# VectorE's order in the first stage of a retention and SSD block, written out by hand

## The chip, the cores and the metric

The kernel runs on one core of a Trainium2 chip. The metric is the time of one execution on the device in microseconds; the time before is the median of three runs. Its engines are TensorE (PE in the profile; PEld is its loading of weights), VectorE (DVE), ScalarE (ACT), GpSimd (POOL) and SyncE (SP), each with a queue of its own that it works off in order. The tile framework places the instructions: a scheduler takes the code's instructions with their dependences and priorities and fixes, when the kernel is built, the order on every engine.

## The reference, cut to what matters

One residual block on 512 tokens of width 2048: a normalization, one combined input projection, a retention branch (8 heads with rotary q and k), a Mamba-2 SSD branch, projections of both, gates, an output projection and a final normalization.

```python
def rmsnorm(x, w):
    xf = x.astype(f32)
    y = xf * lax.rsqrt(jnp.mean(xf * xf, axis=-1, keepdims=True) + EPS)
    return (y * w.astype(f32)).astype(x.dtype)

def rope(t, positions):
    half = t.shape[-1] // 2
    inv_freq = ROPE_THETA ** (-jnp.arange(half, dtype=f32) / half)
    ang = positions.astype(f32)[..., None] * inv_freq
    cos, sin = jnp.cos(ang)[:, :, None, :], jnp.sin(ang)[:, :, None, :]
    t1, t2 = t[..., :half], t[..., half:]
    return jnp.concatenate([t1 * cos - t2 * sin, t2 * cos + t1 * sin], axis=-1)
...
        h = rmsnorm(x, norm1_w[l])
        proj = jnp.einsum('bsd,de->bse', h, w_in[l])
        q, k, v, g_ret, z, xbc, dt_raw, gate_r, gate_s = jnp.split(proj, offsets, axis=-1)
        y_r = (retention(q, k, v, positions) * jax.nn.silu(g_ret.astype(f32))).astype(x.dtype)
        y_s = ssd(xbc, dt_raw, conv_w[l], conv_b[l], dt_bias[l], a_log[l], d_skip[l])
```

The order within the first stage matters here: the normalization of x, its split into operands for TensorE, the tables of cosine and sine (`rope`), the dt projection (`dt_raw`), and the first head's v, q, k and gate.

## The kernel before, in words

All projections are made in units of 256 output columns by 512 tokens, with features on the partitions. The 2048 features are eight *feature pairs* (`r0` to `r7`, each two rows of 128 features by 512 tokens). A number is held as a rounded high part and a low part that is the rest, and a product is three matmuls: high weight by high operand (L213), high by low (L214), low by high (L215). The weights of a unit come by `SP.dma_start` into `wf` (three buffers of two pairs); ScalarE casts the high part `whi` (L148) and VectorE subtracts for the low part `wlo` (L149), seven and six buffers.

A unit is either *plain* (12 matmuls of 512 columns per pair) or uses seven products in place of eight (21 matmuls of 256 columns per pair). The plain one needs only the *first half* of a pair's operand, tile `a` (rows 0 to 3: the difference of two rows, a cast, a low part). The seven-product unit also needs the *second half*, tile `b` (two sums and a difference into `g`, a cast, a low part), and combinations of the weights (L230, L232, L233 on VectorE). Each unit sums into four banks `pb0` to `pb3` of which there is one set, so the next unit's first product on a bank waits until VectorE and ScalarE have read that bank into `o`.

The first stage, in the code's order: `raw` pairs are loaded, ScalarE squares each, VectorE adds its two rows, TensorE sums over features with a matrix of ones (tile `att`); `inverse_root` gives `R1`; the dt weights `wdt` (in tile `e7`, loaded from ScalarE's queue) are scaled by the norm's weights and multiplied with the raw pairs; then each pair is scaled by weight and `R1`, and its first half is made. Head 0 follows with the units V (values), Q and K, all plain, and G (gate), which uses seven products and is the first to need second halves. `rotary_tables` makes the cosine and sine tables in 36 VectorE steps, a generator that the code advances with `step(n)`; `rotate` applies them to q and k, after which TensorE makes the scores.

Two things set the order here. Instructions issued through `InOrder` wrappers (`pe`, `act`, `dve`; in the profile they all have line L118, that of the helper) stay in the order of the code among themselves. Those issued through the plain names (`PE`, `ACT`, `DVE`) are placed where the scheduler finds them best. Before, `first_half` in this stage goes through `dve`, while the second halves and the rotary steps behind the root go through plain `DVE` (the class `Either` switches `vector.now` at the end of the first halves), so the scheduler mixes them in.

Transfers are counted on eight counters, dealt out in turn in the scheduler's order (in the rows below `DMAHW0_49` to `DMAHW7_49`). A transfer is issued only after the one before it on the same counter has landed; its engine's queue shows that as a wait ahead of the issue.

Of the kernel before, what the change touches and what calls it, by code (L numbers as in the profile page):

```python
# [8 lines left out]
F32 = mybir.dt.float32  # L9
# [7 lines left out]
P = 128  # L17
# [6 lines left out]
SH = 64  # L24
# [103 lines left out]
def hybrid_block(tc, A, out):  # L128
# [40 lines left out]
    def first_half(i, DVE=DVE, ACT=ACT):  # L169

        f, t = R[i], hp.tile([P, 8, 256], F32R, name=f"a{i}", tag=f"a{i}")
        X[i] = [t, None]
        DVE.tensor_tensor(f[:, 4, :], f[:, 0, :], f[:, 1, :], op=ALU.subtract)
        ACT.copy(t[:, 0:4, :], f[:, 1:5, :])
        DVE.tensor_tensor(t[:, 4:8, :], f[:, 1:5, :], t[:, 0:4, :].bitcast(F32), op=ALU.subtract)

    def second_halves(room):

        for i in range(NP):
            f, g = R[i], room[i % 2]  # L180
            DVE.tensor_tensor(g[:, 0:2, :], f[:, 0:5:4, :], f[:, 2:3, :].to_broadcast([P, 2, 256]), op=ALU.add)
            DVE.tensor_tensor(g[:, 2, :], f[:, 3, :], g[:, 1, :], op=ALU.subtract)
            t = X[i][1] = hp.tile([P, 6, 256], F32R, name=f"b{i}", tag=f"b{i}")
            split(t[:, 0:3, :], t[:, 3:6, :], g)

# [6 lines left out]
    def load_operands(src, n=NP):  # L192


        for i in range(NP):
            if i < n:
                SP.dma_start(out=raw_tile(i), in_=rows(src, i))
            first_half(i)

# [170 lines left out]
    act.dma_start(out=angles[:, 0, :].bitcast(I32), in_=A["positions"].partition_broadcast(P))  # L370
    act.dma_start(out=wdt, in_=w_in[:, DTO:DTO + SH].rearrange("(k p) c -> p k c", p=P))
    for i in range(NP):
        SP.dma_start(out=raw[i], in_=rows(A["xT"], i))
        if i == 0:
            SP.dma_start(out=cc, in_=A["consts"])

    class Either:

        now = dve

        def __getattr__(self, name):
            return getattr(self.now, name)

    vector = Either()
    steps = rotary_tables(angles, rooms[0][:, 6:8, :].rearrange("p h t -> p (h t)"), vector)

# [5 lines left out]
    act.activation(rstd[:, :1], eps, AF.Abs_reciprocal_sqrt)  # L392
    step(2)
    ps = att_tile()
    for i in range(NP):
        x, y = raw[i], early[i][:, 2 * T:].rearrange("p (r t) -> p r t", r=2)
        if i < NP - 1:
            act.activation(y, x, AF.Square)
            dve.tensor_tensor(y[:, 0, :], y[:, 0, :], y[:, 1, :], op=ALU.add)
            pe.matmul(ps, ones, y[:, 0, :], start=(i == 0), stop=False)  # L400
            step(1)
        else:
            for r in range(2):
                act.activation(y[:, r, :], x[:, r, :], AF.Square)
                pe.matmul(ps, ones, y[:, r, :], start=False, stop=(r == 1))

    dve.tensor_tensor(wdt, wdt, nw[:, :, None].to_broadcast([P, KD, SH]), op=ALU.mult)
    step(2)
    inverse_root(R1, ps, early[1][:, :T], early[2][:, :T], D, dve, act)
# [11 lines left out]

    for i in range(NP):
        for r in range(2):
            x, k = raw[i][:, r, :], 2 * i + r
            dve.scalar_tensor_tensor(x, x, nw[:, k:k + 1], R1, op0=ALU.mult, op1=ALU.mult)
        first_half(i, dve, act)
    vector.now = DVE

# [56 lines left out]
    with tc.tile_pool(name="ret", bufs=1) as rp:  # L485
# [3 lines left out]
        for h in range(NH):  # L489
# [30 lines left out]
            if h == 0:  # L520
                values()
                gs = rp.tile([P, 2, 3, 256], F32, name="g", tag="g")
                second_halves([gs[:, n] for n in range(2)])
                for _ in steps:
                    pass
            q = rotate(QO, qk[:, 0])
# [316 lines left out]
```

## Time and profile before

| what | us |
|---|---|
| time before, median of 3 runs | 2768.85 (2766.91 to 2770.41) |
| profiled execution, its own time | 2769.07 |
| its span | 2767.2 |
| TensorE busy | 2699.1 (98%) |
| VectorE busy | 2371.0 (86%) |
| ScalarE busy | 1343.0 (49%) |
| GpSimd busy | 175.2 (6%) |

The profile names instructions by line, engine, operation and tile, with buffer numbers left out; its records are of one execution. Rows of the timeline begin with the start and the length in us; an "x8" counts instructions that were merged into a row, and a bracket gives the idle time before and what ended it. Rows of waits give the total, the count and the longest. TensorE shows two records for a matmul in plain float32 and one for a rounded one.

### The profile page before, as it was taken

The numbers are of one execution on the slowest core, as the hardware profiler recorded it, in microseconds if no ns is written. First come the engines' busy times: TensorE is split into PE (matmuls) and PEld (weight loads), VectorE is DVE, ScalarE is ACT, GpSimd is POOL, SyncE is SP. The second block draws the span as 40 slices with busy tenths as digits, with TensorE's granted clock in tenths as the row PEclk, the third lists the DMA queues.
The fourth block names the chain that finished last, engine by engine and source line by source line (L and its number), as shares of the span: only waits on it lengthen the run. The fifth ranks groups of instructions, "written<-read, shape, count | busy, mean of one in ns | idle before, by whom it ended". The sixth has DMA issues, their size and how long they took to land.

```text
span 2767.2 us, 51984 instructions
## 1 busy us (share of the span) xinstructions
PE 2699.1 (98%) x20448; PEld 2567.6 (93%) x20448; DVE 2371.0 (86%) x3799; ACT 1343.0 (49%) x1923; POOL 175.2 (6%) x130
## 2 busy tenths in 40 slices
PE   6999999999999999999999999999999999999998
PEld 3799999999999999999999999999999989899898
DVE  8788888888878898898989888898889798898997
ACT  4334333343336555566565556556564353433453
POOL 0000000000000100000000000000000000011221
PEclk8999999999999999999999999999999999999999
DMA  4233333333333434343443434344464544557634
GB/s 141 77 96 92 115 100 107 96 100 103 104 112 107 141 108 127 121 129 121 128 142 120 136 108 128 116 132 126 131 200 144 192 155 141 179 169 230 203 123 138
DMA packets 339766, 362.46 MB, mean 131 GB/s; under 512 B 25152, under 2 KB 297792, under 8 KB 339520
## 3 DMA queue, kind: packets, MB, share of 16 engines
q1 hardware_dynamic: 319136, 325.05, 38.2%
q10 hardware_dynamic: 20384, 34.09, 3.3%
q8 instruction: 160, 2.62, 0.4%
q14 instruction: 86, 0.70, 0.1%
HBM read 321.56 MB, written 37.49 MB: 130 GB/s over the span
## 4 chain that ended last, share of the span: by engine, by line
PE 75%; DVE 11%; DMA 8%; issue 3%; ACT 1%; SPq 1%; POOL 0%; DVEq 0%; ACTq 0%; POOLq 0%
PE pb L215 21%; PE pb L214 21%; PE pb L213 20%; DVE wlo L149 3%; DMA wf<-in_w_in_dram 3%; DMA wf<-in_w_br_ssd_dram 2%; PE att L215 2%; PE att L214 2%; PE att L213 2%; PE att L549 1%; PE att L534 1%; DVE wf L230 1%; PE att L666 1%; PE pb L118 1%; PE att L670 1%
## 5 line engine op out<-in xcount | busy, mean ns | idle before, releaser
L148 ACT CAST whi<-wf 128x896 fp32r<-128x896 f32 (+1 forms) x968 | 818.5, 884 | 925.8 <-PE pb L214 390.0
L149 DVE TENSOR_TENSOR wlo<-wf,whi 128x896 fp32r<-128x896 f32 (+1 forms) x968 | 989.9, 1034 | 64.4 <-ACT whi L148 33.3
L213 PE MATMUL pb<-a,whi 128*128 128x256 f32 (+1 forms) x3328 | 1001.8, 304 | 13.7 <-ACT a L118 9.4
L214 PE MATMUL pb<-a,whi 128*128 128x256 f32 (+1 forms) x3328 | 1002.4, 302 | 8.7 <-DVE a L118 8.7
L215 PE MATMUL pb<-a,wlo 128*128 128x256 f32 (+1 forms) x3328 | 999.6, 302 | 5.9 <-DVE wlo L149 5.9
L213 PEld LDWEIGHTS pb<-a,whi 128*128 128x128 f32 x3328 | 636.7, 192 | 41.5 <-ACT a L118 13.3
L214 PEld LDWEIGHTS pb<-a,whi 128*128 128x128 f32 x3328 | 639.1, 192 | 33.9 <-DVE a L118 12.8
L215 PEld LDWEIGHTS pb<-a,wlo 128*128 128x128 f32 x3328 | 637.9, 192 | 29.9 <-DVE wlo L149 7.7
L213 PE MATMUL pb<-b,whi 128*128 128x256 f32 x2112 | 599.6, 284 | 0.0
L215 PE MATMUL pb<-b,wlo 128*128 128x256 f32 x2112 | 598.8, 284 | 0.0
L214 PE MATMUL pb<-b,whi 128*128 128x256 f32 x2112 | 598.0, 284 | 0.0
L230 DVE TENSOR_TENSOR wf<-wf 128x512 f32<-128x512 f32 x400 | 286.2, 715 | 185.3 <-DMA wf<-in_w_in_dram 138.7
L214 PEld LDWEIGHTS pb<-b,whi 128*128 128x128 f32 x2112 | 405.4, 192 | 0.1
L215 PEld LDWEIGHTS pb<-b,wlo 128*128 128x128 f32 x2112 | 405.3, 192 | 0.2
L213 PEld LDWEIGHTS pb<-b,whi 128*128 128x128 f32 x2112 | 405.4, 192 | 0.0
L233 DVE TENSOR_TENSOR wf<-wf 128x256 f32<-128x256 f32 x400 | 175.5, 439 | 3.4
L232 DVE TENSOR_TENSOR wf<-wf 128x256 f32<-128x256 f32 x400 | 174.5, 436 | 3.6
L215 PE MATMUL att<-a,wlo 128*128 128x256 f32 (+1 forms) x480 | 144.6, 306 | 5.3 <-DVE wlo L149 5.3
L213 PE MATMUL att<-a,whi 128*128 128x256 f32 (+1 forms) x480 | 145.5, 305 | 0.0
L214 PE MATMUL att<-a,whi 128*128 128x256 f32 (+1 forms) x480 | 145.3, 305 | 0.0
L215 PEld LDWEIGHTS att<-a,wlo 128*128 128x128 f32 x480 | 91.0, 192 | 10.3 <-DVE wlo L149 6.5
L659 ACT ACTIVATE L<-L,sst 128x128 f32<-128x128 f32 x256 | 78.5, 390 | 35.8 <-DMA L<-A_d 35.8
(221 smaller groups left out, 2736.6 us busy)
## 6 DMA issues: line engine op xcount, KB each, us to landing
wf<-in_w_in_dram SPq DMA_DIRECT2D x640, 256.0 KB, 3.1
wf<-in_w_br_ssd_dram SPq DMA_DIRECT2D x128, 256.0 KB, 3.4
wf<-in_w_out_dram SPq DMA_DIRECT2D x72, 256.0 KB, 3.2
wf<-in_w_in_dram SPq DMA_DIRECT2D x128, 128.0 KB, 2.6
L<-A_d SPq DMA_DIRECT2D x32, 512.0 KB, 3.7
wf<-in_w_br_ret_dram SPq DMA_DIRECT2D x64, 256.0 KB, 3.4
ys_d<-B ACTq DMA_DIRECT2D x32, 256.0 KB, 2.1
r<-ys_d SPq DMA_DIRECT2D x16, 512.0 KB, 6.1
```

The source lines that it names most:

```text
L118: ins = getattr(self.engine, name)(*args, **kw).ins
L148: ACT.copy(dst_hi, src)
L149: DVE.tensor_tensor(dst_lo, src, dst_hi.bitcast(F32), op=ALU.subtract)
L213: PE.matmul(o, wh, xh, start=b not in started, stop=False, skip_group_check=True)
L214: PE.matmul(o, wh, xl, start=False, stop=False, skip_group_check=True)
L215: PE.matmul(o, wl, xh, start=False, stop=(k == NP - 1), skip_group_check=True)
L230: DVE.tensor_tensor(f2[:, :, 4:6, :], f2[:, :, 1:3, :], f2[:, :, 0:1, :].to_broadcast([P, 2, 2, P]), op=ALU.subtract)
L232: DVE.tensor_tensor(f2[:, :, 0, :], f2[:, :, 2, :], f2[:, :, 4, :], op=ALU.add)
L233: DVE.tensor_tensor(f2[:, :, 6, :], f2[:, :, 3, :], f2[:, :, 0, :], op=ALU.subtract)
L534: PE.matmul(ps[:, :n], k[:, i, sb * P:(sb + 1) * P], q[:, i, sb * P:], start=(i == 0), stop=(i == 1))
L549: PE.matmul(ps[:, :DK], pt[sb][:, (lb - sb) * P:(lb - sb + 1) * P], v[:, sb, :], start=(sb == 0), stop=(sb == lb))
L659: ACT.activation(L[:, i, c, :], L[:, i, c, :], AF.Relu, scale=-1.0, bias=At[:, c, h0 + i:h0 + i + 1])
```

## The change

The order on VectorE is written out. `first_half` and the new `second_half` become generators that stop before and after the low part. After the root, a pair ahead is scaled, subtracted and cast while the low part of the pair before is made, all through `dve`. Second halves and four rotary steps in turn follow through `dve` behind all first halves, after V's code. One rotary step less is taken ahead of the squares, none beside pair 0, and the two steps ahead of the root are gone. The load of `wdt` moves from the head of ScalarE's queue to behind pair 4's square.

```diff
     def first_half(i, DVE=DVE, ACT=ACT):
...
         DVE.tensor_tensor(f[:, 4, :], f[:, 0, :], f[:, 1, :], op=ALU.subtract)
         ACT.copy(t[:, 0:4, :], f[:, 1:5, :])
+        yield
         DVE.tensor_tensor(t[:, 4:8, :], f[:, 1:5, :], t[:, 0:4, :].bitcast(F32), op=ALU.subtract)
+        yield
+
+    def second_half(i, g, DVE=DVE, ACT=ACT):
+
+        f = R[i]
+        DVE.tensor_tensor(g[:, 0:2, :], f[:, 0:5:4, :], f[:, 2:3, :].to_broadcast([P, 2, 256]), op=ALU.add)
+        DVE.tensor_tensor(g[:, 2, :], f[:, 3, :], g[:, 1, :], op=ALU.subtract)
+        t = X[i][1] = hp.tile([P, 6, 256], F32R, name=f"b{i}", tag=f"b{i}")
+        ACT.copy(t[:, 0:3, :], g)
+        yield
+        DVE.tensor_tensor(t[:, 3:6, :], g, t[:, 0:3, :].bitcast(F32), op=ALU.subtract)
+        yield
 
     def second_halves(room):
-
         for i in range(NP):
-            f, g = R[i], room[i % 2]
...
-            split(t[:, 0:3, :], t[:, 3:6, :], g)
+            list(second_half(i, room[i % 2]))
...
-            first_half(i)
+            list(first_half(i))
...
     act.dma_start(out=angles[:, 0, :].bitcast(I32), in_=A["positions"].partition_broadcast(P))
-    act.dma_start(out=wdt, in_=w_in[:, DTO:DTO + SH].rearrange("(k p) c -> p k c", p=P))
...
-    steps = rotary_tables(angles, rooms[0][:, 6:8, :].rearrange("p h t -> p (h t)"), vector)
+    steps = rotary_tables(angles, rooms[0][:, 6:8, :].rearrange("p h t -> p (h t)"), dve)
...
-    step(2)
+    step(1)
     ps = att_tile()
     for i in range(NP):
...
-            step(1)
+            if i:
+                step(1)
+            if i == 4:
+                act.dma_start(out=wdt, in_=w_in[:, DTO:DTO + SH].rearrange("(k p) c -> p k c", p=P))
...
     dve.tensor_tensor(wdt, wdt, nw[:, :, None].to_broadcast([P, KD, SH]), op=ALU.mult)
-    step(2)
     inverse_root(R1, ps, early[1][:, :T], early[2][:, :T], D, dve, act)
...
-    for i in range(NP):
+    def normalized(i):
         for r in range(2):
             x, k = raw[i][:, r, :], 2 * i + r
             dve.scalar_tensor_tensor(x, x, nw[:, k:k + 1], R1, op0=ALU.mult, op1=ALU.mult)
-        first_half(i, dve, act)
-    vector.now = DVE
+        yield from first_half(i, dve, act)
+
+    ahead = [normalized(i) for i in range(NP)]
+    next(ahead[0])
+    for i in range(NP):
+        if i + 1 < NP:
+            next(ahead[i + 1])
+        next(ahead[i])
...
                 values()
                 gs = rp.tile([P, 2, 3, 256], F32, name="g", tag="g")
-                second_halves([gs[:, n] for n in range(2)])
-                for _ in steps:
-                    pass
+                ahead = [second_half(i, gs[:, i % 2], dve) for i in range(NP)]
+                next(ahead[0])
+                for i in range(NP):
+                    if i + 1 < NP:
+                        next(ahead[i + 1])
+                    next(ahead[i])
+                    step(4)
+                step(99)
```

Three places in the built order. Names have their buffer's number behind them; the changed kernel's lines are eight and more further down (L213 to L215 become L221 to L223, L534 becomes L545). First, ScalarE at the start, before, with what each row waits for:

```order
L118 DMA B8_122<-in_positions_dram 128x512
L118 DMA e7_112<-in_w_in_dram 128x16x64
L118 ACT_TABLE_LOAD
L118 ACTIVATE rstd_80<-eps_91 128x1 [waits Pool_49]
L118 ACTIVATE e0_105<-r0_113 128x1024 [waits DMAHW2_49]
```

and changed, from pair 4's square (the rows between are the same):

```order
L118 ACTIVATE e4_109<-r4_117 128x1024 [waits DMAHW7_49]
L118 DMA e7_112<-in_w_in_dram 128x16x64 [waits DMAHW4_49]
L118 ACTIVATE e5_110<-r5_118 128x1024 [waits DMAHW0_49]
L118 ACTIVATE e6_111<-r6_119 128x1024 [waits DMAHW1_49]
L118 ACTIVATE e7_112<-r7_120 128x512 [waits DMAHW2_49]
L118 ACTIVATE e7_112<-r7_120 128x512
L148 CAST whi_257<-wf_254 128x512 [waits DMAHW3_49]
L148 CAST whi_273<-wf_254 128x512
L148 CAST whi_292<-wf_289 128x512 [waits DMAHW5_49]
L148 CAST whi_308<-wf_289 128x512 [waits DMAHW6_49]
L118 ACTIVATE e1_106<-att_135,eps_91 128x512 [waits PE_49]
L148 CAST whi_327<-wf_324 128x512 [waits DMAHW0_49]
```

The dt weights' load now has a wait, and three squares, the first weight casts and the root's activation stand behind it. On SyncE, before, the rows that tell the counters are

```order
L373 DMA r6_119<-in_xT_dram 128x2x512 [waits DMAHW2_49]
L373 DMA r7_120<-in_xT_dram 128x2x512 [waits DMAHW3_49]
L227 DMA wf_258<-in_w_in_dram 128x2x256 [waits DMAHW4_49]
L227 DMA wf_258<-in_w_in_dram 128x2x256 [waits DMAHW5_49]
L435 DMA na_1115<-in_a_log_dram 128x64 [waits DMAHW4_49]
```

and changed

```order
L380 DMA r6_119<-in_xT_dram 128x2x512 [waits DMAHW1_49]
L380 DMA r7_120<-in_xT_dram 128x2x512 [waits DMAHW2_49]
L235 DMA wf_254<-in_w_in_dram 128x2x256 [waits DMAHW3_49]
L235 DMA wf_254<-in_w_in_dram 128x2x256 [waits DMAHW4_49]
L441 DMA na_1115<-in_a_log_dram 128x64 [waits DMAHW3_49]
```

Before, counter 3 was that of the dt weights' load, and the last pair `r7` waits for it. Now the load comes after `na` in the dealing, so it has counter 4, whose last user is the second transfer of the first weight tile.

Second, VectorE behind the root (`R1`), before:

```order
L118 SCALAR_TENSOR_TENSOR R1_81<-R1_81,e1_106 128x512
L347 TENSOR_TENSOR B8_122<-B8_122,A8_121 128x512
L118 SCALAR_TENSOR_TENSOR r0_113<-r0_113,nw_76,R1_81 128x512 x2
L337 CAST B8_122<-B8_122 128x512
L118 TENSOR_TENSOR r0_113<-r0_113 128x256
L419 COPY rstd_80<-att_196 128x4
L338 TENSOR_TENSOR B8_122<-B8_122 128x512
L181 TENSOR_TENSOR g_417<-r0_113 128x512
L344 TENSOR_SCALAR B8_122<-B8_122 128x512
L118 TENSOR_TENSOR a0_204<-r0_113,a0_204 128x1024
L118 SCALAR_TENSOR_TENSOR r1_114<-r1_114,nw_76,R1_81 128x512 x2
L182 TENSOR_TENSOR g_417<-r0_113,g_417 128x256
```

and changed, from the fifth weight's low part:

```order
L149 TENSOR_TENSOR wlo_328<-wf_324,whi_327 128x512
L149 TENSOR_TENSOR wlo_344<-wf_324,whi_343 128x512
L118 TENSOR_TENSOR e7_112<-e7_112,nw_76 128x1024
L118 TENSOR_SCALAR e2_107<-att_135 128x512
L118 TENSOR_TENSOR R1_81<-e1_106 128x512
L118 SCALAR_TENSOR_TENSOR R1_81<-R1_81,e2_107 128x512
L118 SCALAR_TENSOR_TENSOR R1_81<-R1_81,e1_106 128x512
L118 SCALAR_TENSOR_TENSOR r0_113<-r0_113,nw_76,R1_81 128x512 x2
L118 TENSOR_TENSOR r0_113<-r0_113 128x256
L118 SCALAR_TENSOR_TENSOR r1_114<-r1_114,nw_76,R1_81 128x512 x2
L118 TENSOR_TENSOR r1_114<-r1_114 128x256
L118 TENSOR_TENSOR a0_200<-r0_113,a0_200 128x1024
```

Rotary steps (on `A8`, `B8`) and second halves (on `g`) are gone from between the pairs, and six weights' low parts stand ahead of the scaling of the dt weights (`e7`), which stood ahead of all of them.

Third, TensorE at the scores of head 0 (`att<-B8`), before, at the first of their two places, among the products of pairs 2 and 3 of G (`pb2_818`, `pb3_819`):

```order
L214 MATMUL pb3_819<-b2_430,whi_882 128x256
L534 MATMUL att_800<-B8_122 128x512
L534 MATMUL att_804<-B8_122 128x384
L534 MATMUL att_808<-B8_122 128x256
L534 MATMUL att_812<-B8_122 128x128
L215 MATMUL pb3_819<-b2_430,wlo_883 128x256
```

and changed, where `pb0_1177` is the first bank of the unit behind G:

```order
L221 MATMUL pb0_1177<-a2_211,whi_1243 128x256
L222 MATMUL pb0_1177<-a2_211,whi_1243 128x256
L545 MATMUL att_800<-B8_122 128x512 x2
L545 MATMUL att_804<-B8_122 128x384 x2
L545 MATMUL att_808<-B8_122 128x256 x2
L545 MATMUL att_812<-B8_122 128x128 x2
L223 MATMUL pb0_1177<-a2_211,wlo_1244 128x256
```

The scores moved from inside G to behind it and eight products of the next unit.

More of the change, by code (lines that the diff above doesn't have):

```diff
@@ L174, in first_half @@
         ACT.copy(t[:, 0:4, :], f[:, 1:5, :])
+        yield
         DVE.tensor_tensor(t[:, 4:8, :], f[:, 1:5, :], t[:, 0:4, :].bitcast(F32), op=ALU.subtract)
+        yield
[8 more added lines that the diff above has]
+        yield
     def second_halves(room):
         for i in range(NP):
-            f, g = R[i], room[i % 2]
-            DVE.tensor_tensor(g[:, 0:2, :], f[:, 0:5:4, :], f[:, 2:3, :].to_broadcast([P, 2, 256]), op=ALU.add)
-            DVE.tensor_tensor(g[:, 2, :], f[:, 3, :], g[:, 1, :], op=ALU.subtract)
-            t = X[i][1] = hp.tile([P, 6, 256], F32R, name=f"b{i}", tag=f"b{i}")
-            split(t[:, 0:3, :], t[:, 3:6, :], g)
+            list(second_half(i, room[i % 2]))
     def pair_rows(f):
@@ L375, in hybrid_block @@
             SP.dma_start(out=cc, in_=A["consts"])
[L377 to L384, printed above, removed]
-    steps = rotary_tables(angles, rooms[0][:, 6:8, :].rearrange("p h t -> p (h t)"), vector)
+    steps = rotary_tables(angles, rooms[0][:, 6:8, :].rearrange("p h t -> p (h t)"), dve)
     def step(n):
```

## The prediction

> **What bounds the kernel now.** I read the page first, then TensorE's waits by stretch, then the stretches themselves, then the first 85 us instruction by instruction. The page's span and busy row:
>
> ```profile
> span 2767.2 us, 51984 instructions
> PE 2699.1 (98%) x20448; PEld 2567.6 (93%) x20448; DVE 2371.0 (86%) x3799; ACT 1343.0 (49%) x1923; POOL 175.2 (6%) x130
> ```
>
> TensorE is busy for all but 68 us, so only a stretch in which it waits or runs slowly can give much. Such a stretch is the first unit, V. Its waits, then (third row) all that TensorE waits for from 84.5 to 300 us:
>
> ```profile
> PE pb L213 <- ACT a L118: 9.4, 7, 2.5
> PE pb L214 <- DVE a L118: 8.7, 7, 1.9
> ...
> PE pb L215 <- DVE wlo L149: 1.3, 1, 1.3
> ```
>
> The stretches (columns: length, busy time and count of PE, PEld, DVE, ACT, POOL, granted clock, DMA share, GB/s):
>
> ```profile
> 29.50:33.10 3.60, 1.10 (x10) 0.97 (x8) 3.60 (x8) 1.63 (x2) 0.00 (x0) 1.00 0.29 100
> 33.10:84.50 51.40, 35.74 (x96) 23.20 (x97) 49.26 (x81) 20.95 (x28) 0.00 (x0) 0.77 0.10 31
> 84.50:107.00 22.50, 22.50 (x104) 18.71 (x103) 9.15 (x16) 6.77 (x13) 0.00 (x0) 1.00 0.23 71
> 107.00:129.00 22.00, 22.00 (x98) 18.21 (x97) 18.08 (x31) 7.61 (x11) 0.00 (x0) 1.00 0.32 96
> 129.00:153.50 24.50, 24.50 (x186) 22.88 (x185) 20.30 (x33) 7.64 (x10) 0.00 (x0) 1.00 0.28 86
> ```
>
> In V (33.1 to 84.5) VectorE is busy 49.26 of 51.40 us, TensorE 35.74 at a clock of 0.77. VectorE is the bound there, and nowhere else near: the Q, K and G units that follow keep TensorE full at clock 1.00. The three rows of waits say the same: 18.1 us in V, 1.3 in the next 215. So the forecast is a date: the first product of Q, at 84.54 now. TensorE's order behind the first two heads is the same but for a late stretch in the output projection, so the end moves by what that date moves, less any wait newly made behind it.
>
> **The change, part by part.** One: the dt weights' load leaves the head of ScalarE's queue. What it did there, and what stands around it:
>
> ```profile
> SPq L373 <- DMA e<-in_w_in_dram: 6.6, 1, 6.6
> ...
> e<-in_w_in_dram ACTq DMA_DIRECT2D x1, 512.0 KB, 12.9
> ```
> ```profile
> 1.18 0.47 ACTq L118 DMA_DIRECT2D e<-in_w_in_dram  x1
> 15.22 1.06 ACT L118 ACTIVATE e<-r 128x1024 f32<-128x1024 f32 x1 [0.36 <-DMA r<-in_xT_dram]
> 16.56 1.06 ACT L118 ACTIVATE e<-r 128x1024 f32<-128x1024 f32 x1 [0.29 <-DMA r<-in_xT_dram]
> 19.29 1.15 ACT L118 ACTIVATE e<-r 128x512 f32<-128x512 f32 x2 [0.32 <-DMA r<-in_xT_dram]
> 19.75 2.84 PE L118 MATMUL att<-e,cc 128*128 128x512 f32 x6 [0.23 <-DVE e L118]
> 20.22 1.22 DVE L118 TENSOR_TENSOR e<-e,nw 128x1024 f32<-128x1024 f32 x1
> 20.35 2.54 ACT L148 CAST whi<-wf 128x512 fp32r<-128x512 f32 x4
> 21.36 0.42 DVE L118 CAST B<-B 128x512 int32<-128x512 f32 x1
> 22.53 7.09 PE L118 MATMUL att<-r,e 128*64 128x512 f32 x32
> 22.80 0.68 ACT L118 ACTIVATE e<-att,eps 128x512 f32<-128x512 f32 x1
> 23.64 1.32 ACT L148 CAST whi<-wf 128x512 fp32r<-128x512 f32 x2 [0.16 <-DMA wf<-in_w_in_dram]
> 28.64 0.68 DVE L118 SCALAR_TENSOR_TENSOR R<-R,e 128x512 f32<-128x512 f32 x1
> 29.55 1.05 PE L118 MATMUL att<-cc,R 128*128 128x2 f32 x8
> 33.12 1.85 PE L213 MATMUL pb<-a,whi 128*128 128x512 f32 x4 [2.52 <-ACT a L118]
> ```
>
> The load took 12.9 us beside the features, in 256-byte rows, and SyncE waited 6.6 us for it before it could issue the last feature pair, since a transfer is issued only when the one before it on its counter has landed. In the changed order the load stands behind the square of pair 4, and the counter that it gets was last used by the second transfer of the first weight tile (the orders above). So ScalarE, in its queue's order, stops at this issue until that transfer has landed. When is that? Feature pairs land 1.34 to 1.37 us apart (starts 15.22, 16.56, 19.29 of squares that wait for them: 4.07 for three), so half a megabyte taken out from between them is worth 1.4 us; 2.8, an estimate, if the load's 256-byte rows move at half that pace. I take 2.0. The last pair then lands at 19.29 - 2.0 = 17.3 and two quarter-megabyte transfers later, at 18.7, ScalarE goes on: issue 0.47, 19.2. Pair 5 was squared at 16.56, so the squares of the last three pairs are 2.6 us late: done at 19.2 + 2 x 1.06 + 1.15 = 22.5.
>
> TensorE has by then had nothing for about 5 us. What a wait does to its pace is seen at the start of V:
>
> ```profile
> 36.17 0.63 PE L215 MATMUL pb<-a,wlo 128*128 128x512 f32 x1
> 36.60 0.50 PE L214 MATMUL pb<-a,whi 128*128 128x512 f32 x1
> 36.94 0.39 PE L215 MATMUL pb<-a,wlo 128*128 128x512 f32 x1
> 37.17 0.39 PE L214 MATMUL pb<-a,whi 128*128 128x512 f32 x1
> 84.54 0.44 PE L213 MATMUL pb<-a,whi 128*128 128x512 f32 x1
> ```
>
> Starts lie 0.43 apart until 36.60, then 0.34, then 0.23: after the wait before 33.12 the products ran at half pace for 3.5 us, a loss of 1.75. [...]
>
> Bounds for the sum of squares: pair 5's sum starts at 19.2 + 1.06 + 0.7 = 20.95, and four sums at 0.9 (19.75: three in 2.84) end at 24.6, at half pace throughout at 28.2; with a loss of 1.75, at 26.4. Then the root's activation (0.2 + 0.68), two weight casts (1.32) and their low part on VectorE (0.1 + 0.60), because six low parts now stand ahead of the dt weights' scaling: 29.35. The load, issued at 19.2, lands by 32.1 if it takes 12.9 again; its neighbours now have 1 KB rows instead of 2 KB and there are fewer of them, so I take about 8 and do not let it decide; 32.1 stays as an end. So scaling starts at 29.35 (27.5 to 32.1), where it was 20.22: the start loses 9 us.
>
> Two: from there VectorE is free of the rest. Scaling 1.14 (20.22 to 21.36), three steps of the root at 0.60 and one of 0.68: R1 at 33.0 instead of 29.3. TensorE: dt product from 30.7, 7.02 (22.53 to 29.55) + 1.75 for the clock, then 1.05: first product of V at 40.5, against 33.12.
>
> Three: V itself. VectorE's work for a pair, start to start:
>
> ```profile
> 39.60 1.21 DVE L118 TENSOR_TENSOR a<-r,a 128x1024 fp32r<-128x1024 f32 x1
> 40.73 1.40 DVE L118 SCALAR_TENSOR_TENSOR r<-r,nw,R 128x512 f32<-128x512 f32 x2
> 42.06 0.68 DVE L149 TENSOR_TENSOR wlo<-wf,whi 128x512 fp32r<-128x512 f32 x1
> 42.66 0.41 DVE L182 TENSOR_TENSOR g<-r,g 128x256 f32<-128x256 f32 x1
> 43.60 0.41 DVE L118 TENSOR_TENSOR r<-r 128x256 f32<-128x256 f32 x1
> 43.93 0.68 DVE L149 TENSOR_TENSOR wlo<-wf,whi 128x512 fp32r<-128x512 f32 x1
> ```
>
> Low part 1.13, normalizing two rows 1.33, a weight's low part 0.60, difference 0.33: 3.4 us per pair, 8 x 2.79 + 6 x 0.60 = 25.9 from 33.0, last low part at 58.9. Before, a pair took 51.40 / 8 = 6.4 us because second halves and rotary steps lay between. TensorE's 96 products at 0.23 take 22.1: 40.5 + 22.1 = 62.6, later than VectorE's 58.9 plus the last eight products (1.8). So TensorE is the later one, no longer waits, and stays at full pace. Q's first product needs the first bank emptied; VectorE comes to it after the first second half, 0.60 + 0.33 + 0.60 + 0.60 + 0.33 + 0.87 + 0.60 + 0.42 behind 58.9 with one wait for V's seventh pair, about 63.5. **Gain so far: 84.54 - 63.5 = 21.0.**
>
> Four: what was moved must be done somewhere.
>
> ```profile
> L149 DVE TENSOR_TENSOR b<-g,b 128x768 fp32r<-128x768 f32 x8 | 7.6, 946 | 0.9 <-ACT b L148 0.9
> L181 DVE TENSOR_TENSOR g<-r 128x512 f32<-128x512 f32 x8 | 5.4, 677 | 0.0
> L182 DVE TENSOR_TENSOR g<-r,g 128x256 f32<-128x256 f32 x8 | 3.3, 410 | 0.0
> ```
>
> Second halves: 7.6 + 5.4 + 3.3 = 16.3. Rotary steps behind V: 29 by the changed order, 18 long at 0.68 and 11 short at 0.41, 16.7. Records overlap by 0.08, so 33.0 less 53 x 0.08: 28.8 us of VectorE. They are covered by its idle time in Q, K and G: 22.50 - 9.15, 22.00 - 18.08 and 24.50 - 20.30 make 21.5. The rest, 7.3, is still owed when G ends. But TensorE's order now has the scores of the first head behind G and eight products of the next unit, not inside G. Adding up starts along the changed order, the rotated k is ready 1 us after TensorE comes to the scores, and a second wait of about 1 stands at the first head's transposes. I take 2 us, between 0 and 7.3; the low end because the weights' parts, on which the products wait, stand interleaved with the moved steps and come in time by 2 to 8 us. ScalarE's casts of the second halves fall into a stage where it is busy 6.77 to 7.64 of 22 to 24.5 us and cost nothing. SyncE's weight loads follow the freeing of buffers as before; GpSimd's queue is unchanged.
>
> Sum, against the profiled execution's 2769.07 (0.22 above the median of 2768.85): -21.0 + 2 = -19.0, **2750**.
>
> **The rivals.** *ScalarE is not held by the load's issue.* Then the squares end at 18.6, and the sixth weight's low part and the load decide: about 26 instead of 29.35, 3.4 us earlier, 2746.7. For it: no row shows ScalarE waiting to issue; against: SyncE's 6.6 us. [...]
>
> *The moved work finds only part of the room.* VectorE's idle time in Q and K is waiting inside its own order, for TensorE, and a step that stands behind such a wait can't use it. With 5.5 us more to wait than I take, all the 7.3: 2755.5; with a few more, 2760.
>
> *The same, to the full, ends slower.* Place: the rotation of q and k, ahead of the scores. If none of the 21.5 us could be used, TensorE would wait all 28.8: 2769.07 - 21.0 + 28.8 = 2777. It turns slower by 0.2% when the waits pass 26.5. Against it: the moved steps stand between the waits, most of them with no wait of their own.
>
> *TensorE keeps V's mean pace*, because something other than the waits slows it. 35.74 us busy for 96 products is 0.37 each; V would take 35.7 from 40.5, Q come at 77, and the end at 2769.07 - 7.5 + 2 = 2763.5; at half pace throughout, 41.3 and 2769. For it: the clock of 0.77 beside waits of 2.5 us at most. Against it: rows 36.17 to 36.94, where 3.5 us without a wait end the half pace, and the clock of 1.00 in all stretches that do not wait. [...] That the change doesn't do what it says is excluded by the order.
>
> **How the numbers follow.** Forecast 0.66, unheld ScalarE 0.14, part of the room 0.11, V's mean pace 0.05, slower 0.04. The ends: start at 27.5 and no new wait, 2750 - 1.9 - 2 = 2746, or 2745 with the unheld ScalarE; start at 32.1 and all of 7.3, 2750 + 2.75 + 5.3 = 2758. Differences under 0.2% (5.5 us, about what a measurement of this kernel tells from none) are "same": faster 0.90, same 0.06, slower 0.04.
>
> **What would show it.** Right: a wait of ScalarE of 4 to 5 us before the square of pair 5; the scaling of the dt weights near 29; first product of V near 40, its clock near 1.00; Q's first product near 63.5; TensorE's wait for rotated k under 3 us. Wrong: TensorE waiting in V for features again, or waits for VectorE in K and G adding up to more than 7.

## The result, and the profile after

The changed kernel takes 2748.91 us (median of 6 runs, 2745.81 to 2755.9) where the kernel before takes 2767.4 (6 runs, 2765.62 to 2770.41): ratio 0.9939, 95% interval 0.9927 to 0.9951. The forecast was 2750, range 2745 to 2758. The profiled execution of after is its longest, 2755.9 us, so its late stages are not typical; the first 300 us, on which the forecast rests, are read from it.

The page's span and busy row, then how the start went (timeline: start, length, engine, line, operation; in brackets the idle time before it and what ended it):

```profile
span 2754.0 us, 51975 instructions
PE 2691.5 (98%) x20448; PEld 2565.0 (93%) x20448; DVE 2368.3 (86%) x3799; ACT 1342.7 (49%) x1923; POOL 179.3 (7%) x130
```
```profile
18.39 0.39 ACTq L118 DMA_DIRECT2D e<-in_w_in_dram  x1
18.83 3.04 ACT L118 ACTIVATE e<-r 128x1024 f32<-128x1024 f32 x4 [5.01 <-DMA wf<-in_w_in_dram]
20.66 6.51 PE L118 MATMUL att<-e,cc 128*128 128x512 f32 x8 [4.94 <-DVE e L118]
28.44 1.29 DVE L149 TENSOR_TENSOR wlo<-wf,whi 128x512 fp32r<-128x512 f32 x2 [3.53 <-ACT whi L148]
29.65 1.22 DVE L118 TENSOR_TENSOR e<-e,nw 128x1024 f32<-128x1024 f32 x1
30.92 9.88 PE L118 MATMUL att<-r,e 128*64 128x512 f32 x32 [3.75 <-DVE e L118]
41.65 1.18 PE L221 MATMUL pb<-a,whi 128*128 128x512 f32 x4
...
65.30 0.50 PE L221 MATMUL pb<-a,whi 128*128 128x512 f32 x1 [1.62 <-DVE o L270]
```

ScalarE stops 5.01 us, not for its own data but for a weight transfer (`wf`), and goes on when it has issued the dt weights' load at 18.39. The squares, their sum (20.66), the scaling (29.65, before: 20.22), the dt product and V's first product (41.65, before: 33.12) are late one after the other. Yet Q's first product comes at 65.30, where it came at 84.54. In between, the stretches of V, Q, K and G and the attention behind them (columns as before the change: length, busy time and count of PE, PEld, DVE, ACT, POOL, clock, DMA share, GB/s) and all that TensorE waits for from 64 to 300 us:

```profile
41.60:63.50 21.90, 21.90 (x98) 17.97 (x97) 20.87 (x34) 10.70 (x15) 0.00 (x0) 1.00 0.24 73
63.50:86.00 22.50, 20.88 (x96) 17.25 (x96) 21.33 (x38) 8.48 (x14) 0.00 (x0) 1.00 0.23 71
86.00:108.00 22.00, 22.00 (x98) 18.22 (x98) 21.69 (x39) 9.46 (x13) 0.00 (x0) 1.00 0.31 96
108.00:128.00 20.00, 20.00 (x161) 19.65 (x161) 19.57 (x33) 8.38 (x10) 0.00 (x0) 1.00 0.33 100
128.00:160.00 32.00, 29.38 (x208) 26.66 (x207) 26.80 (x57) 13.97 (x20) 2.20 (x4) 1.00 0.23 70
```
```profile
PE att L572 <- ACT yn L570: 2.0, 3, 1.1
PE pb L221 <- DVE o L270: 1.6, 1, 1.6
PE pb L221 <- ACT o L274: 0.9, 1, 0.9
```

V is now 21.9 us long, full, at clock 1.00 (before: 51.4 us, 35.74 busy, 0.77). VectorE, which was busy for 9.15 us of 22.5 in Q and 18.08 of 22 in K, is now busy 21.33 of 22.5 there and 21.69 of 22: the second halves and the rotary steps are done where TensorE has work of its own. For that TensorE waits 4.5 us behind V up to 300 us, 1.3 before.

### The profile page after: what moved, and what is told of

Read it like the earlier page. It is cut to its first block, busy times and chain, and to the rows that moved or that the text cites. A ratio compares the mean times of both kernels' runs of the same rounds, so it can differ in the third digit from the quotient of the medians.

```text
span 2754.0 us, 51975 instructions
## 1 busy us (share of the span) xinstructions
PE 2691.5 (98%) x20448; PEld 2565.0 (93%) x20448; DVE 2368.3 (86%) x3799; ACT 1342.7 (49%) x1923; POOL 179.3 (7%) x130
## 4 chain that ended last, share of the span: by engine, by line
PE 78%; DVE 9%; DMA 6%; issue 3%; ACT 1%; SPq 1%; POOL 0%; DVEq 0%; ACTq 0%; POOLq 0%
PE pb L223 21%; PE pb L221 21%; PE pb L222 21%; DMA wf<-in_w_in_dram 3%; DVE wlo L149 3%; PE att L222 2%; PE att L223 2%; PE att L221 2%; PE att L545 1%; DVE wf L238 1%; PE att L560 1%; PE att L677 1%; DMA wf<-in_w_br_ssd_dram 1%; PE att L681 1%; PE pb L118 1%
## 5 line engine op out<-in xcount | busy, mean ns | idle before, releaser
L221 PE MATMUL pb<-a,whi 128*128 128x256 f32 (+1 forms) x3328 | 998.3, 303 | 7.7 <-DVE o L277 4.3
L223 PE MATMUL pb<-a,wlo 128*128 128x256 f32 (+1 forms) x3328 | 994.5, 301 | 7.2 <-DVE wlo L149 7.1
L221 PEld LDWEIGHTS pb<-a,whi 128*128 128x128 f32 x3328 | 636.0, 191 | 32.3 <-issue 7.4
L223 PEld LDWEIGHTS pb<-a,wlo 128*128 128x128 f32 x3328 | 635.2, 191 | 30.4 <-DVE wlo L149 8.9
L221 PE MATMUL pb<-b,whi 128*128 128x256 f32 x2112 | 600.1, 284 | 0.0
L223 PE MATMUL pb<-b,wlo 128*128 128x256 f32 x2112 | 599.0, 284 | 0.0
L221 PEld LDWEIGHTS pb<-b,whi 128*128 128x128 f32 x2112 | 405.8, 192 | 0.1
L223 PEld LDWEIGHTS pb<-b,wlo 128*128 128x128 f32 x2112 | 405.5, 192 | 0.2
L223 PE MATMUL att<-a,wlo 128*128 128x256 f32 (+1 forms) x480 | 144.5, 306 | 5.1 <-DVE wlo L149 5.1
L221 PE MATMUL att<-a,whi 128*128 128x256 f32 (+1 forms) x480 | 145.2, 305 | 0.0
L223 PEld LDWEIGHTS att<-a,wlo 128*128 128x128 f32 x480 | 90.8, 192 | 10.3 <-DVE wlo L149 6.5
L221 PEld LDWEIGHTS att<-a,whi 128*128 128x128 f32 x480 | 92.0, 192 | 3.9
```

What stands on the lines that cost most here:

```text
L221: PE.matmul(o, wh, xh, start=b not in started, stop=False, skip_group_check=True)
L223: PE.matmul(o, wl, xh, start=False, stop=(k == NP - 1), skip_group_check=True)
```

## The experiments

Times are compared as ratios to the kernel before on the same chip in the same session, since chips differ by a few us (its medians lie between 2763.06 and 2767.4). "First V" and "first Q" are the starts of those units' first products; "ahead" is how much sooner than in the profile of before TensorE starts the product that is the program's 1500th there, counted from 0 (276.48 us), with added products not counted.

| kernel | first V | first Q | ahead | median us | ratio, 95% interval |
|---|---|---|---|---|---|
| before | 33.12 | 84.54 | 0 | | 1 |
| after | 41.65 | 65.30 | 16.7 | 2748.91 | 0.9939 (0.9927 to 0.9951) |
| e1 load at the head, as before | 30.70 | 58.17 | 23.1 | 2743.02 | 0.9914 (0.9901 to 0.9927) |
| e2 load on SyncE | 29.60 | 57.27 | 25.9 | 2741.32 | 0.9912 (0.9896 to 0.9927) |
| e3 load behind the last square | 35.61 | 59.28 | 22.7 | 2744.85 | 0.9924 (0.9911 to 0.9937) |
| e4 before, load moved alone | 42.14 | 89.03 | -3.5 | 2767.16 | 1.0007 (0.9999 to 1.0016) |
| e5 before, V's products twice | 32.87 | 85.39 | -2.0 | 2762.5 | 0.9995 (0.9986 to 1.0005) |
| e6 after, rotary steps between | 40.99 | 79.76 | 5.5 | 2761.84 | 0.9995 (0.9986 to 1.0004) |
| e7 after, second halves not fixed | 40.99 | 71.68 | 13.5 | 2749.9 | 0.9957 (0.9943 to 0.9970) |
| e8 after, 19 useless products | 43.62 | 67.40 | 16.8 | 2737.66 | 0.9912 (0.9899 to 0.9926) |
| e9 after, one small product | 37.59 | 62.97 | 18.9 | 2748.11 | 0.9937 (0.9923 to 0.9950) |
| e10 after, 9 useless products | 35.74 | 61.76 | 22.4 | 2740.25 | 0.9909 (0.9895 to 0.9922) |
| e11 e2, low parts on GpSimd | 32.51 | 61.03 | 21.4 | 2744.59 | 0.9922 (0.9909 to 0.9934) |
| e12 e8 again | 43.41 | 67.19 | 17.2 | 2739.07 | 0.9910 (0.9896 to 0.9923) |

The lead at the 1500th product and the gain by the ratio (of the session's median before) agree within about 4 us, which is also what an interval spans to either side. Only e8 and e12 are off by more, 7.5 and 7.7 us.

**Where the load stands (e1 to e4).** e1 puts it back, e2 gives it to SyncE, e3 leaves it to ScalarE but later; e4 makes this move alone in the kernel before.

```diff
# e1: at the head, behind the load of the positions
+    act.dma_start(out=wdt, ...)
# e2: behind the loop that loads the feature pairs
+    SP.dma_start(out=wdt, ...)
# e3: behind the loop of squares
+    act.dma_start(out=wdt, ...)
# e1, e2, e3; in e4 these lines are added to before instead
-            if i == 4:
-                act.dma_start(out=wdt, ...)
```

> The order of VectorE is kept, and only the dt weights' load goes back to the head of ScalarE's queue. Theory (the changed order gains in V, the moved load loses at the start): ScalarE's wait of 5.0 us before the fifth pair's square is gone, the dt weights are scaled near 20.2 as before the change (29.65 after it), V's first product comes near 33 (41.65), V takes TensorE the same 21.6, Q's first product comes near 57.5 (65.30), and the time is 2748.9 - 8 = about 2741. SyncE waits again about 6.6 us for this load before the last feature pair. Rival (the start doesn't matter, since VectorE then has to do the moved work in Q, K and G and TensorE waits there longer by what was gained): 2746 to 2749.

> The order of VectorE is kept, and the dt weights' load is issued by SyncE behind the eight feature pairs and ahead of the first weight tile, by neither end of ScalarE's queue. Theory (ScalarE's stop was the loss): the squares end at 18.8 as the last pair lands at 17.1; the load lands 3 to 6 us behind the last pair, 20 to 23, scaling starts then, V's first product 33 to 36, Q's first product 57 to 60: 2741 to 2744. The first weight tile lands 1.4 to 2.8 us later, which is hidden. Rival (the weights become the bound instead): V waits for its first weights, and the time is 2746 to 2749.

> The order of VectorE is kept, and the load stays in ScalarE's queue, but behind the last square instead of behind the fifth. Its counter was last used by the same weight transfer, which has landed by then (18.3). Theory (ScalarE stopped for that counter): no wait of 5 us, squares end at 18.8 instead of 23.1; the load is issued at 18.9 and lands near 24.5 to 25, scaling starts near 25 (29.65), V's first product near 37 (41.65), the time is 2749 - 4.6 = 2744. Rival (the issue itself stops ScalarE, wherever it stands): the wait of about 5 us is found behind the last square, the casts of the first weights are late, and the time stays within 1.5 us of 2749.

> The kernel before with the load alone moved behind the fifth square; VectorE's order is as before. Theory (V is bound by VectorE, whose work starts when R1 is there): R1 comes 4.3 us later (33.6 for 29.3), V's and all that follows end 4.3 later, about 2771.7; V's first product near 41, Q's near 89, the clock in V about 0.77 to 0.85. Rival (TensorE's own pace bounds V): 8.5 us later, 2776. Rival (the start has slack): 2767 to 2768.

Timelines of e1, e2 and e3, in this order (scaling of the dt weights, V's first product; in e1 SyncE's wait last, in e3 the load's issue first and the dt product between):

```profile
20.20 1.22 DVE L118 TENSOR_TENSOR e<-e,nw 128x1024 f32<-128x1024 f32 x1
30.70 1.18 PE L221 MATMUL pb<-a,whi 128*128 128x512 f32 x4
SPq L381 <- DMA e<-in_w_in_dram: 6.6, 1, 6.6
```
```profile
19.02 1.23 DVE L118 TENSOR_TENSOR e<-e,nw 128x1024 f32<-128x1024 f32 x1 [1.70 <-DMA e<-in_w_in_dram]
29.60 2.08 PE L221 MATMUL pb<-a,whi 128*128 128x512 f32 x4 [1.22 <-ACT a L118]
```
```profile
18.32 0.40 ACTq L118 DMA_DIRECT2D e<-in_w_in_dram  x1
24.69 1.23 DVE L118 TENSOR_TENSOR e<-e,nw 128x1024 f32<-128x1024 f32 x1 [1.31 <-DMA e<-in_w_in_dram]
25.97 8.80 PE L118 MATMUL att<-r,e 128*64 128x512 f32 x32 [5.87 <-DVE e L118]
35.61 1.17 PE L221 MATMUL pb<-a,whi 128*128 128x512 f32 x4
```

e3 shows what ScalarE stood still for. In the traces the order on TensorE, VectorE and ScalarE is that of after, instruction for instruction; only the issue stands later. In both runs it goes out 0.02 us after the trace has the second transfer of the first weight tile landed: at 18.39 in after (landed at 18.37), at 18.32 in e3 (18.30). In after three squares stand behind it and are late by the wait; in e3 the last square ends at 17.97, and 0.35 us of a stop are left of the 5.0. The stop is the wait for that transfer, and the issue adds little to it (0.39 us). V and Q come 6.0 us sooner than in after, 4 us by the ratios.

In e1 the load is back, SyncE waits its 6.6 us as before the change, and V begins 11 us earlier than in after; the scheduler also puts the scaling (20.20) ahead of the weights' low parts there. So the order of VectorE alone is worth ratio 0.9914, and the moved load took 0.0025 of it back, 7 us (medians: 2748.91 - 2743.02 = 5.9). The two intervals touch at 0.9927, so the size is less sure than the order of events. e2 takes the load off ScalarE's queue and begins V earliest. SyncE's queue does feel it: the four weight issues behind the load take 9.5 us there, 4.6 in after.

V's starts lie 6.0 us apart in e2 and e3, Q's only 2.0. In e1 and e2 TensorE comes early enough to wait for VectorE again (2.1 and 1.5 us); e1 from 30.6 to 57 us, columns as before, and TensorE's waits for first halves:

```profile
30.60:57.00 26.40, 24.17 (x99) 17.48 (x98) 26.36 (x41) 13.13 (x19) 0.00 (x0) 1.00 0.20 61
PE pb L222 <- DVE a L118: 2.1, 6, 0.4
```

The times that I expected of e1, e2 and e3 were met within 3 us, in e1 and e2 in part by luck: V began 2.3 us before the 33 that I had for e1 and 3.4 before the 33 to 36 for e2, and from V's first product to Q's it was 27.5 us in e1, where I had 24.5.

e4 is the other half of this: in the old order the same stop delays V's first product by 9.0 us, Q's by 4.5, and the time by 1.0 us by the medians, at most 4.4 by the interval. Its stretch V, ScalarE's wait and TensorE's longest wait:

```profile
42.10:89.00 46.90, 32.83 (x98) 22.26 (x97) 46.55 (x79) 21.56 (x28) 0.00 (x0) 0.82 0.11 34
ACT e L118 <- DMA wf<-in_w_in_dram: 5.0, 1, 5.0
PE pb L214 <- DVE a L118: 9.5, 5, 2.1
```

V is 46.9 us there, of which VectorE is busy 46.55. I expected Q near 89 and had it (89.03); the time that I expected with it, 2771.7, was set against the 2767.4 of another chip and is 1.0016 of that, the very end of the interval. 3.5 us of it are left at the 1500th product; the profiled execution makes them good between 780 and 980 us, which one trace can't tell from the spread of executions.

**What bounds V (e5).** Each product of V is issued twice in the kernel before.

```diff
             PE.matmul(o, wh, xl, start=False, stop=False, skip_group_check=True)
+            if twice:
+                for y, z in ((wh, xh), (wh, xl), (wl, xh)):
+                    PE.matmul(o, y, z, start=False, stop=False, skip_group_check=True)
```

> The kernel before, with every product of the first unit, V, issued twice (the sums are doubled, so the first head's output is another). TensorE then has 192 products there instead of 96, and nothing else is changed. Theory (V is bound by VectorE, and TensorE's slow clock is a consequence of its waits): V hardly gets longer, since 192 x 0.225 = 43 us fit into 51.4; the last products behind the last low part are 24 instead of 12, so Q comes 2 to 6 us later, and the time is 2768 to 2773; the granted clock in V rises from 0.77 to above 0.9. Rival (TensorE keeps V's mean pace of 0.37 us a product for another reason than its waits): 96 x 0.37 = 35.7 us more work, 71.5 us busy in V, so Q comes 20 us or more later: 2786 to 2802 at a clock near 0.77.

V in e5, columns as before:

```profile
32.90:85.40 52.50, 47.38 (x193) 36.77 (x194) 50.34 (x83) 22.09 (x28) 0.00 (x0) 0.97 0.10 31
```

TensorE does twice the work in V, 47.38 us busy instead of 35.74, and V is 52.5 us long instead of 51.4. Its clock is 0.97 instead of 0.77. So TensorE's slow pace in the old V was a result of waiting for VectorE and cost nothing; removing 96 of 192 products would gain nothing there. The rival, 20 us or more, is out. Even my 2 to 6 us for the longer tail were too much.

**Which of the moved parts (e6, e7).** One is put back in each.

```diff
# e6
             next(ahead[i + 1])
         next(ahead[i])
+        step(4)
...
-                    step(4)
                 step(99)
# e7
-                ahead = [second_half(i, gs[:, i % 2], dve) for i in range(NP)]
...
+                second_halves([gs[:, n] for n in range(2)])
                 step(99)
```

> The changed kernel with the rotary steps put back between the pairs of first halves, four to a pair, the second halves staying behind all first halves. Theory (V is as long as VectorE's work in it): 29 steps, 14.6 us, come back into V: VectorE is done at 33.6 + 25.9 + 14.6 = 74, Q's first product comes near 76 to 77 (65.30 in the changed kernel), TensorE waits in V again; behind V 14.6 us less of VectorE's work is owed, and waits of up to 3 us in the first head go. The time is 2749 + 11 - 2 = 2758 (2755 to 2761). Rival (the rotary steps fit into VectorE's slack, since TensorE takes 21.6 us and VectorE 25.9 from an earlier start): 2749 to 2752.

> The changed kernel with the second halves not in the fixed order but left to be placed by the scheduler, as before the change, and the rotary steps behind V. By its order five second halves then lie in V, 4 x 0.87 + 5 x 0.60 + 4 x 0.33 = 7.8 us. Theory: VectorE is done with the first halves at 33.6 + 25.9 + 7.8 = 67.3, Q's first product comes near 70 (65.30), the time is 2749 + 5 = 2754, less up to 2 of waits. Rival (there is slack for them): 2747 to 2750.

V in e6 and then in e7, each with the longest row of TensorE's waits from 29 to 300 us:

```profile
41.00:79.70 38.70, 26.67 (x98) 19.84 (x97) 37.40 (x62) 14.49 (x19) 0.00 (x0) 0.91 0.13 41
PE pb L222 <- DVE a L118: 12.0, 5, 3.4
```
```profile
41.00:71.60 30.60, 24.64 (x98) 18.75 (x98) 30.52 (x48) 14.67 (x20) 0.00 (x0) 0.94 0.17 52
PE pb L222 <- DVE a L118: 6.0, 4, 1.9
```

With the rotary steps between the pairs TensorE waits 12.0 us for first halves again, V is 38.7 us and the gain is gone (0.9995); at Q 14.5 us are lost, 3 more than expected, and the interval lies above my 2755 to 2761 by ratio (of 2767.4, 0.9955 to 0.9977). Of the 5.5 us of lead that e6 still has at the 1500th product the interval leaves 3.9 at most. e7 lost 6.4 us at Q (4.7 expected), 3.2 by the 1500th product and 0.0018 in ratio, which the two intervals can't tell from nothing. In both VectorE is busy nearly all of V (37.40 of 38.7, 30.52 of 30.6): V is as long as what stands in VectorE's queue ahead of the last first half.

**What the half pace at the start costs (e8 to e10, e12).** Useless products fill TensorE's two waits.

```diff
# e8, e12: n = 11 and 8, into a bank of its own; e10: 5 and 4, into the dt product's bank
+    def keep_busy(n, y):
+        for _ in range(n):
+            pe.matmul(warm, ones, y, start=True, stop=True)
...
             if i == 4:
                 act.dma_start(out=wdt, ...)
+                keep_busy(11, y[:, 0, :])
...
                 pe.matmul(ps, ones, y[:, r, :], start=False, stop=(r == 1))
+    keep_busy(8, early[6][:, 2 * T:3 * T])
# e9, in place of these: one product of 128 columns into a bank of its own
+                pe.matmul(extra[:, :P], ones, y[:, 0, :P], start=True, stop=True)
```

> The changed kernel with 19 products of no use on TensorE, written to a bank that nobody reads: 11 of them behind the sum of pair 4's squares, where TensorE waits 4.9 us, and 8 behind the last sum, where it waits 3.7. Theory (half pace after these waits costs the start 3 us in the sum of squares and 2.9 in the dt product): the sum takes about 3.4 instead of 6.51, the dt product 7.1 instead of 9.88, V's first product comes 5 to 6 us earlier than 41.65, near 36; the time is 2749 - 5 = 2744, or 2746 where V then waits for VectorE. Rival (the clock is lowered whether or not TensorE is kept busy): sum and dt product as long as before, 2749 or up to 1 slower.

> The changed kernel with one small product of no use (128 columns) behind the sum of pair 4's squares, written to a PSUM bank of its own from the pool of four that the later stages take in turn. The order on all engines is otherwise that of the changed kernel; only which of the four banks each later tile gets is moved on by one. It asks where the gain of the run with 19 useless products came from: its first head began no earlier than the changed kernel's (16.8 us ahead of the kernel before at TensorE's 1500th product, as against 16.7), and it was 29 ahead at the end. Theory (the banks' turn): the gain comes without keeping TensorE busy; sum of squares and dt product as slow as in the changed kernel, TensorE's waits between 780 and 1110 us shrink from 3.5 us to about 1, ratio 0.991 to 0.992. Rival (run to run and chip to chip differences in these stages): ratio 0.994, as the changed kernel.

> The changed kernel with 9 products of no use instead of 19, since each took 0.87 us at full pace and not 0.43: 5 behind the sum of pair 4's squares (4.3 us of a wait of 4.9) and 4 behind the last sum (3.5 of 3.7), written to the bank of the dt product, so that the later tiles get the banks that they get in the changed kernel. Theory (half pace after these waits costs the start 3 us in the sum and 2.9 in the dt product): sum of squares over near 24.6 (27.2), dt product from 28 to 35.3 (30.92 to 40.8), V's first product near 36.4 (41.65), Q's first near 60 (65.30): 5.3 us, ratio 0.992. Rival (V then waits for VectorE, whose work starts with R1 only 2.8 earlier): Q's first near 62.5, ratio 0.993.

> The kernel with 19 useless products (e8) once more, unchanged. There V's first product (43.62) and Q's (67.40) came 2 us later than in the changed kernel (41.65, 65.30), and yet the ratio was 0.9912 against 0.9939. Theory (the end follows Q's first product, and the low ratio was the spread between sets of runs): Q's first product near 67 again, ratio 0.993 to 0.995. Rival (something behind the first head is faster in this program): ratio 0.990 to 0.992 again, with the gain between TensorE's 5500th product and the end.

e10 and then e9 (a product of 512 columns with the ones is two matmuls here, so x16 holds four useless products of two each and the last four sums):

```profile
20.40 7.48 PE L118 MATMUL att<-e,cc 128*128 128x512 f32 x16 [0.62 <-DVE e L118]
27.81 7.09 PE L118 MATMUL att<-r,e 128*64 128x512 f32 x32
35.74 1.16 PE L221 MATMUL pb<-a,whi 128*128 128x512 f32 x4
```
```profile
20.52 5.40 PE L118 MATMUL att<-e,cc 128*128 128x512 f32 x8 [4.31 <-DVE e L118]
29.66 7.09 PE L118 MATMUL att<-r,e 128*64 128x512 f32 x32 [3.75 <-DVE e L118]
37.59 1.17 PE L221 MATMUL pb<-a,whi 128*128 128x512 f32 x4
```

In e10 the dt product takes 7.09 us instead of 9.88, V begins 5.9 us earlier and Q 3.5, because V then waits for VectorE (four times 0.36 to 0.39); between my two cases. So the half pace behind the stop costs the changed kernel 3.5 us at Q, and 5.7 by the 1500th product, since the wait for `yn` has shrunk too (0.2 for 2.0). The ratio, 0.9909 against 0.9939, says 8; part of that may be what e8 and e12 show below. One small product (e9) already saves the dt product's half pace in this execution, and the ratio doesn't show it.

e8 was mis-sized (a product took 0.87 us, so its 16.5 us overfilled the waits), and V and Q came 2 us later than in after. Still its ratio is 0.9912, and e12 gave 0.9910 on another chip. I had expected e12 to fall back to 0.994; it didn't. e9 rules out the banks' turn (0.9937). The gain lies behind the first head. The stretches 750 to 1100 and 1100 to 2300 us of after, then of e8 and e12:

```profile
750.00:1100.00 350.00, 344.71 (x2715) 331.31 (x2714) 292.59 (x471) 195.69 (x305) 23.30 (x19) 1.00 0.41 123
1100.00:2300.00 1200.00, 1193.02 (x9219) 1143.86 (x9219) 1047.19 (x1639) 665.20 (x985) 67.47 (x49) 1.00 0.44 137
```
```profile
750.00:1100.00 350.00, 349.19 (x2752) 336.17 (x2751) 295.82 (x477) 198.86 (x310) 24.71 (x19) 1.00 0.41 124
1100.00:2300.00 1200.00, 1196.28 (x9262) 1148.11 (x9261) 1053.20 (x1647) 665.61 (x985) 66.91 (x49) 1.00 0.44 137
```
```profile
750.00:1100.00 350.00, 348.45 (x2750) 335.55 (x2749) 294.40 (x476) 198.30 (x309) 24.77 (x19) 1.00 0.41 123
1100.00:2300.00 1200.00, 1196.93 (x9265) 1148.78 (x9264) 1053.22 (x1647) 665.29 (x984) 66.71 (x49) 1.00 0.44 138
```

TensorE is idle 7.7 us less in e8 (349.19 - 344.71 + 1196.28 - 1193.02) and as much less in e12. The instructions' order there is that of after on TensorE, VectorE and ScalarE. Why these waits are shorter stays open; it is not an earlier start. The traces alone would not settle it: e4 and e5 gain 3.6 and 4.2 us on the kernel before between 780 and 980 us, with the order of before there. What speaks for a real gain is the two ratios, just clear of that of after.

**A try at a still better version (e11).** e2 with the low parts of V's weights on GpSimd.

```diff
-        DVE.tensor_tensor(dst_lo, src, dst_hi.bitcast(F32), op=ALU.subtract)
+        eng.tensor_tensor(dst_lo, src, dst_hi.bitcast(F32), op=ALU.subtract)   # POOL in the first unit, V
```

> The kernel with the load on SyncE's queue (e2), and the low parts of V's eight weight pieces subtracted by GpSimd instead of VectorE. VectorE loses 8 x 0.6 = 4.8 us in and before V; GpSimd is idle there, and its other operations of this size take 1.6 us. Theory (VectorE's work in V still sets V's pace in e2, by six waits of 0.3 to 0.4 us and the late start of the normalization): R1 comes 2.4 us earlier, V's first product near 27 (29.60), V takes 22 us, Q's first product near 51 (57.27), ratio 0.9890 against 0.9912. Rival (GpSimd takes 3.2 us for each, as in its slowest group of this size, or slows VectorE beside it): TensorE waits for low parts, Q's first product 57 to 60, ratio 0.9912 or more.

Groups of instructions from 15 to 60 us (count, busy time, mean ns), of e2 and then of e11:

```profile
L118 DVE SCALAR_TENSOR_TENSOR r<-r,nw,R 128x512 f32<-128x512 f32 x16 | 11.3, 748 | 0.0
L118 DVE SCALAR_TENSOR_TENSOR R<-R,e 128x512 f32<-128x512 f32 x2 | 1.4, 684 | 0.0
```
```profile
L118 DVE SCALAR_TENSOR_TENSOR r<-r,nw,R 128x512 f32<-128x512 f32 x16 | 15.1, 984 | 0.1
L118 DVE SCALAR_TENSOR_TENSOR R<-R,e 128x512 f32<-128x512 f32 x2 | 3.3, 1649 | 0.1
L149 POOL TENSOR_TENSOR wlo<-wf,whi 128x512 fp32r<-128x512 f32 x8 | 13.3, 1684 | 27.8 <-ACT whi L148 20.5 <-PE pb L223 7.3
```

GpSimd needs 1.68 us for each, as the theory had it, but VectorE's own instructions get longer beside it: the steps of the root 1649 ns instead of 684, the normalizations 984 instead of 748 on average. V begins 2.9 us later than in e2, and Q 3.8, at 61.03. The rival's second half was right in that VectorE is slowed; but TensorE waits for the first operand (`a`, 4.1 us), not for low parts, and Q comes behind the rival's 57 to 60.

## Why the prediction was right, point by point

- *ScalarE is held by the load's issue*: right. Predicted issue 18.7, seen 18.39; a wait of 4 to 5 us was named, 5.01 seen; e3 shows the cause. The rival "not held" was priced at 3.4 us; with the load behind the last square (e3) it is 6.0 us at Q and 0.0015 of ratio, 4 us, and with no stop at all (e1) 7. For the load's 256-byte rows half the features' pace was assumed; in the trace of before one took 18.4 ns in the mean and a feature's row of 2048 bytes 91.1, so it was 0.62 of that pace. In e3, with the load behind all pairs, the last squares start at 16.82, 2.5 us sooner than before the change (19.29), where I took 2.0.
- *Half pace after the stop*: a loss of 1.75 us each for the sum and the dt product was mis-sized. The sum ended at 27.17 (predicted 26.4) and the dt product took 9.88 (8.77): by the trace's record of the clock the half pace lasted 6.8 us each time (from 19.53 and from 29.77), not 3.5, and 5.7 of them fell into each: a loss of 2.8 us. Six low parts ahead of the scaling, 29.35 predicted, 29.65 seen, hid the first error by luck, as ScalarE and VectorE took less for the last two weights than I allowed. V's first product came at 41.65, not 40.5.
- *V without waits at full pace, 22.1 us*: right; 41.65 to the last product at 63.29 is 21.6. e5, e6 and e7 show from three sides that VectorE's queue had set V's length.
- *Q's first product at 63.5*: 65.30. TensorE waits 1.6 us there for VectorE to read the first bank; I had left 0.9 between V and Q. VectorE comes to that read by the predicted steps, 4.5 us behind its last low part of a first half, but this one ended at 60.8 instead of 58.9: `R1` was 0.5 us late (33.52), and at 58.0 VectorE stood still for 1.0 us ahead of a weight's low part, whose cast had waited for TensorE's products, and these had begun 1.15 us late. Gain at Q 19.24, not 21.0.
- *New waits 2 us*: of the right size, 19.24 - 16.7 = 2.5 by the 1500th product. Of the two places that I named, the wait for the rotated k isn't there and the transposes' is (`yn`, 2.0, not 1); 0.9 us for a bank (L274) I didn't name.
- *The sum*: -19.0 predicted, -18.5 by the medians of one session (0.0061 of 2767.4 is 16.9; the interval is 13.6 to 20.2). The profiled execution alone, 2769.07 to 2755.9, would have said 13.2: the rest was lost after 2400 us in that execution, not in the first head. That 2748.91 lies 1 us from 2750 is in part luck: by the 1500th product and by the ratio the gain is near 17, 2 us short of the sum.
- *TensorE keeps V's mean pace* (2763.5 or 2769) and *the moved work finds no room* (2777): out, by the clock of 1.00 in V and by TensorE's waits of 4.5 us. The second rival has a slip: all the 7.3 is 5.3 us more than the 2 taken, not 5.5, and gives 2755.4.

What the prediction undervalued is how the two halves of the change compare. It booked 9 us for the late start as the price of the whole; e1 shows that the changed order didn't need it.

## What to carry to other kernels

Find the engine whose queue sets a stage's length, and count only what stands in that queue ahead of the last thing the next engine needs: doubling the other engine's work (e5) moved Q by 0.9 us and starting it 6.0 us later (e3 against e2) by 2.0, but work put back into that queue moved it by all its length (e6, 14.5). A transfer's issue stood in ScalarE's queue and stopped the three squares behind it for 5.0 us (after); ask which transfer it must wait for, and try it a few instructions later (e3, 0.35 us of the stop left) or on another queue (e2, V's first product 12 us sooner). Price a stall on TensorE with the half pace around it (6.8 us each time in after, 2.8 us lost in the sum and in the dt product each), and settle differences of a few us by ratios from the same chip, not by one profile each.

## What the runs showed of the hardware

By the trace's record of the clock each stretch of TensorE at half pace in before and after, but the idle end of the program, is 3.41 or 6.83 us long, and the starts of one run's stretches lie a whole number of 3.41 us apart (after: 19.53, 29.77, 2528.32, 2596.59 and 2606.83). TensorE was not idle ahead of each of them. Two neighbouring stretches of the kernel before, of which the second is at half pace:

```profile
43.65:47.05 3.40, 1.19 (x4) 0.67 (x4) 3.40 (x8) 1.45 (x2) 0.00 (x0) 1.00 0.34 104
47.10:50.50 3.40, 2.29 (x5) 1.82 (x6) 3.40 (x6) 0.60 (x1) 0.00 (x0) 0.50 0.15 49
```

TensorE was busy for 1.19 of the 3.4 us ahead of the half pace there. Of two such stretches with 1.55 us busy, from 63.1 us on in e6 and in e7, only that in e7 was followed by half pace (clock 0.50 from 66.5 to 69.9; 1.00 in e6). The busy time alone doesn't settle it: in e9 TensorE was busy for about 1.5 us from 24.45 on, to the end of the sum at 25.92, and the dt product behind took 7.09 us, at full pace; in e2 it was busy for 2.26 us from 26.11 on, to 28.37, and V's first products start 0.43 us apart until 32.77 and 0.23 later. V of the kernel before, whose waits were 2.5 us at most, had five stretches at half pace (from 33.40, 47.06, 60.71, 74.36 and 81.19).

VectorE was slower beside GpSimd in e11: its step of the root took 1649 ns beside subtractions on GpSimd of 1684 ns, and 684 in e2 without them, 2.4 times as long.
